# One decoder layer on one core: the indexer's queries worked out for the last 384 of 512 tokens

## The chip, the cores and the metric

The kernel runs on 1 core of a Trainium2 chip. The metric is the device time of one execution in microseconds (us); lower is better. The engines that the text speaks of are TensorE (PE in the rows; its weight loads are PEld), VectorE (DVE), ScalarE (ACT), GpSimd (POOL), and SyncE (SP), whose queue issues all loads and stores.

## The reference

One decoder layer for 512 tokens of 1024 numbers, all in float32. What the change touches is the sparse attention of branch B. An indexer scores every key for every query, and each query attends only to its best 128 keys:

```
top = min(DSA_MAX_TOPK, s // 4)                       # 128 for s = 512
logits = einsum('qhd,sd->qhs', qii, kf)               # qii: indexer queries, 8 heads of 64
score = einsum('qh,qhs->qs', wi, relu(logits))
score = where(k_pos <= q_pos, score, NEG)
_, idx = lax.top_k(score, top)
ok = idx <= q_pos
```

A query among the first 128 tokens has at most 128 admissible keys, so for it the choice takes all of them, and no score is needed. The scores of the first 128 tokens are never used.

Around it: RMSNorm and one input projection to the heads of two attention branches (MoBA in A, DSA in B), the indexer and two gates; rotary positions on all queries and keys; both attentions; a gated merge and an output projection; then a mixture of 32 experts (two of them per token) with a final RMSNorm.

## The kernel before

**First part (to about 400 us): projections and attention.** The input stands transposed in two float32r parts (`xh`, `xl`) and so do the weights (`wh`, `wl`), so one product takes three matmuls for each of 8 slices `k` (lines 255 to 257 in `proj_T`). A chunk of 256 weight columns makes two blocks of 128 rows by 512 tokens in PSUM (`two_blocks`). For queries and keys `rope_of` turns a block with four VectorE operations (lines 282 to 285), then `q_stack` copies it to a float32r part on ScalarE (line 307) and takes the rest on GpSimd (line 308). The indexer's queries are the chunks `qi0` and `qi1`, four blocks in all.

`attend` works on four quads of heads: a0, a1 (branch A), then b0, b1 (branch B). A quad has 8 steps (2 pairs of heads by 4 blocks of 128 queries). A step multiplies queries with keys (lines 432, 433), makes the softmax on VectorE and ScalarE (lines 436 to 439), transposes (448) and multiplies with the values (460). Between the pieces of a step TensorE does other work, drawn from one long list, `others()`: qi0; then qi1, qa1 and ka1 in turn with the indexer's scores (`idx_scores`, lines 389 to 393); the values vb; qb0, kb0; the merge of branch A (`merge_a`); qb1, kb1; the gates of B. How much is drawn is set by costs that each piece of the list yields (0.64 us for three projection matmuls, line 258) against the figures in `SHARE` (for a0, 9.1 us ahead of the first step and 4.4 us in each of 9). `run_to` draws what must be done before the next quad.

`topk` (lines 397 to 404) finds the 128 best keys with 16 pairs of MAX (402) and MATCH_REPLACE (403) for each of the query blocks 1, 2 and 3, 48 pairs in all on VectorE, and turns the scores (`bias1`, `bias2`, `bias3`) into a mask that b0 and b1 add to their scores (line 436).

**What sets the order.** TensorE's instructions stay in the order in which the program was written. VectorE, ScalarE, GpSimd and SP get theirs from a scheduler that estimates when each operand is ready and fills free places with later work; on the chip each queue then runs in that fixed order.

**Second part (from about 465 us): the experts.** 192 loads of 1 MB (`we`, line 609) bring all expert weights. A load can start only when one of a fixed number of places in SBUF is free; from q = 0 on a place comes free when the matmuls of its piece (lines 860, 867) are done.

Of the kernel before, what the change touches and what calls it, by code (L numbers as in the profile page):

```python
# [10 lines left out]
F32 = mybir.dt.float32  # L11
# [6 lines left out]
ALU = mybir.AluOpType  # L18
# [3 lines left out]
P = 128  # L22
T = 512
D = 1024
NT = T // P
NK = D // P
# [110 lines left out]
def layer_kernel(ctx: ExitStack, tc: tile.TileContext, xT, x, w_ki, w_ch, w_ab, w_out, g_mix, g_ffnk, g_fin, w_r, b_r,  # L137
                 w_e, const, rope, out):
    nc = tc.nc
    pe, act, dve, pool, sp = nc.tensor, nc.scalar, nc.vector, nc.gpsimd, nc.sync  # L140
# [17 lines left out]
    def t2(shape, dtype=F32, name="t2", tag="r"):  # L158
        return temps[tag][0].tile(shape, dtype, tag=tag, name=name, bufs=temps[tag][1])

    def small(shape, name, dtype=F32):
        return sm.tile(shape, dtype, tag=name, name=name)

    def bank(name="mm"):
        return pm.tile([P, 512], F32, tag="mm", name=name)
# [18 lines left out]
    def load_split(src, pair=None, place=None):  # L184
        hi, lo = pair or w_pair()
        for _ in halves_of(hi, lo, src, place):
            pass
        return hi, lo
# [15 lines left out]
    for k in range(NK):  # L204
        if k % 4 == 0:
            next(load_ki)
        r, h, l = xraw[k // 4][:, k % 4], xh[k // 4][:, k % 4], xl[k // 4][:, k % 4]
# [18 lines left out]
    cosr, sinr, cmask = rc[:, 0], rc[:, 1], rc[:, 2]  # L226
# [20 lines left out]
    def xk(k, part):  # L247
        return (xh if part == 0 else xl)[k // 4][:, k % 4]

    def proj_T(w, col, ps, ks=range(NK)):  # L250

        hi, lo = w
        for k in ks:
            a = hi[:, k, col:col + P]
            pe.matmul(ps, a, xk(k, 0), start=k == 0, stop=False)  # L255
            pe.matmul(ps, a, xk(k, 1), start=False, stop=False)  # L256
            pe.matmul(ps, lo[:, k, col:col + P], xk(k, 0), start=False, stop=k == NK - 1)  # L257
            yield 0.64

    done, due = set(), [0.0]  # L260

# [14 lines left out]
            run(gen, 0.3)  # L276
        due[0] = 0.0

    def rope_of(ps, rows=P):

        u, r = t2([rows, T], name="ru"), t2([rows, T], name="r")
        dve.tensor_tensor(r, ps, sinr[:rows], ALU.mult)
        dve.stream_shuffle(u, r, [i ^ 1 for i in range(32)])
        dve.tensor_tensor(ps, ps, cosr[:rows], ALU.mult)
        dve.tensor_tensor(r, ps, u, ALU.add)
        return r

    def chunk(name):
        with tc.high_priority(PRIO):
            return load_split(w_ch[CHUNKS.index(name)])  # L290

    def two_blocks(name):
        w, ps = chunk(name), []
        for b in range(2):
            ps.append(bank())
            yield from proj_T(w, b * P, ps[b])
        return ps

    LOW, UPP = slice(0, 64), slice(64, 128)
# [1 line left out]
    def q_stack(name, ps):  # L301

        qs = Q[name[1:]] = S.get([P, 4, T], F32R, name)
        for b in range(2):
            r = rope_of(ps[b])
            for j, h, l in ((2 * b, LOW, UPP), (2 * b + 1, UPP, LOW)):
                act.copy(qs[h, j], r[h])
                pool.tensor_tensor(qs[l, j], r[h], qs[h, j].bitcast(F32), ALU.subtract)

    def k_stack(name, ps):  # L310

# [48 lines left out]
    S.free(*xtok, junk)  # L360
    run(proj_T(w_k0, P, ps_k[1]))
    q_stack("qa0", ps_q)
    k_stack("ka0", ps_k)

# [259 lines left out]
    for n in range(4):  # L624
# [6 lines left out]
        for b in range(2):  # L631
# [11 lines left out]
            for t in range(NT):  # L643
                mv, h, l = m[:, t * P:(t + 1) * P], mt[t][:, 0, c], mt[t][:, 1, c]
# [4 lines left out]
    for a in range(0, NK, 4):  # L649
        hi, lo = [w[:, a:a + 4] for w in ws[3]]  # L650
# [240 lines left out]
    def silu_of(h1):  # L891
        out = []
        for h in range(2):
            out.append(t2([P, FF], name="silu", tag="silu"))
            act.activation(out[h], h1[h], AF.Silu)  # L895
        return out
# [111 lines left out]
    for q in range(NQ):  # L1008
        if q == last:
# [5 lines left out]
            rv = nc.values_load(cint[0:1, 0:1], min_val=0, max_val=T)  # L1015
# [12 lines left out]
        a = silu_of(h1)  # L1028
# [50 lines left out]
    for t in range(NT):  # L1079
        combine(selT, y, 1, t)  # L1080
        squares(t, 1)
        r = small([P, 1], "fin")
# [59 lines left out]
```

## Time and profile before

| | us |
|---|---|
| median of 3 runs | 941.35 (941.22 to 945.83) |
| profiled execution, its time | 942.32 |
| span of its instructions | 940.4 |
| PE busy | 875.7 |
| DVE busy | 433.8 |
| ACT busy | 278.3 |
| POOL busy | 176.5 |

The span runs from the first to the last instruction; the profiled execution took 1.9 us more than that, and 0.97 us more than the median. PE's busy time overstates its work, because one matmul starts before the one ahead has ended; what a matmul costs is read from start to start. A row of the wait view names the waiting engine and line, then the releaser, the sum, the number of waits and the longest.

### The profile page before, as it was taken

What the parts mean: (1) busy time and instruction counts of PE and PEld (TensorE: products, weight loads), DVE (VectorE), ACT (ScalarE), POOL (GpSimd) and SP (SyncE); (2) the same over time, 40 slices, a digit from 0 to 9 for tenths busy, and PEclk for the clock granted to TensorE, in tenths of its full rate; (3) what the DMA queues carried; (4) which work ended last, traced back from release to release, by engine and by line L of the source; (5) the groups of instructions that cost most, each with busy time, mean ns of one, the idle gap of its engine ahead of it and who ended that gap; (6) DMA issues with size and microseconds to landing.
All of it is one profiled execution on the core that took longest, in us unless ns stands there. A gap on an engine that the chain in (4) does not pass through costs nothing. (4 is left out here: it accounts for less than half of the span.)

```text
span 940.4 us, 15614 instructions
## 1 busy us (share of the span) xinstructions
PE 875.7 (93%) x6436; PEld 517.1 (55%) x6436; DVE 433.8 (46%) x991; ACT 278.3 (30%) x585; POOL 176.5 (19%) x112
## 2 busy tenths in 40 slices
PE   7999999989999999889999999998998989987885
PEld 5897779768777877689834342422423223232221
DVE  4737899998544545941823322231322212213004
ACT  5546654562444544433501000000100000100004
POOL 2495334342214711221200000000000000000003
PEclk9999999999999999899999999999999999999898
DMA  8422112112224223455679999999999999999985
GB/s 330 157 71 67 55 36 90 48 57 77 77 82 180 87 69 112 135 229 228 226 317 421 419 420 421 420 418 422 419 420 420 421 422 419 421 420 419 402 327 217
DMA packets 41118, 244.51 MB, mean 260 GB/s; under 512 B 4944, under 2 KB 5328, under 8 KB 16336
## 3 DMA queue, kind: packets, MB, share of 16 engines
q1 hardware_dynamic: 41040, 243.45, 65.0%
q8 instruction: 52, 0.85, 0.4%
q14 instruction: 26, 0.21, 0.1%
HBM read 241.33 MB, written 2.10 MB: 259 GB/s over the span
## 5 line engine op out<-in xcount | busy, mean ns | idle before, releaser
L860 PE MATMUL h<-we,xs 128*32 128x512 f32 x2048 | 238.4, 601 | 26.3 <-DMA we<-in_w_e_dram 19.4
L860 PEld LDWEIGHTS h<-we,xs 128*32 128x32 f32 x2048 | 59.1, 110 | 180.5 <-issue 117.4
L867 PE MATMUL y<-we,hT 128*32 128x512 f32 x1024 | 116.3, 595 | 5.3 <-DMA we<-in_w_e_dram 5.2
L255 PE MATMUL mm<-xh,wh 128*128 128x512 f32 x272 | 109.9, 404 | 0.8 <-DVE bias L393 0.8
L257 PE MATMUL mm<-xh,wl 128*128 128x512 f32 x272 | 107.5, 395 | 0.0
L256 PE MATMUL mm<-xl,wh 128*128 128x512 f32 x272 | 107.5, 395 | 0.0
L1072 POOL TENSOR_TENSOR fo<-x,gfn 128x512 f32<-128x512 f32 x4 | 5.0, 1282 | 450.0 <-DVE x L927 450.0
L170 POOL TENSOR_TENSOR wl<-raw,wh 128x1024 fp32r<-128x1024 f32 (+1 forms) x23 | 64.5, 2803 | 132.1 <-ACT wh L169 68.5
L927 DVE TENSOR_TENSOR x<-cps,x 128x512 f32<-128x512 f32 x64 | 43.3, 688 | 86.3 <-PE cps L925 86.1
L867 PEld LDWEIGHTS y<-we,hT 128*32 128x32 f32 x1024 | 30.0, 109 | 77.1 <-issue 57.0
L901 DVE SCALAR_TENSOR_TENSOR silu<-silu,gate,h 128x512 f32<-128x512 f32 x16 | 12.0, 747 | 124.5 <-issue 82.8
L257 PEld LDWEIGHTS mm<-xh,wl 128*128 128x128 f32 x272 | 51.1, 188 | 12.6 <-DVE wl L170 0.4
L255 PEld LDWEIGHTS mm<-xh,wh 128*128 128x128 f32 x272 | 51.1, 188 | 11.7 <-issue 1.2
L256 PEld LDWEIGHTS mm<-xl,wh 128*128 128x128 f32 x272 | 51.2, 188 | 9.5
L169 ACT CAST wh<-raw 128x1024 fp32r<-128x1024 f32 (+1 forms) x46 | 45.6, 1028 | 31.9 <-DMA raw<-in_w_ch_dram 13.5
L169 ACT CAST y<-y 128x512 fp32r<-128x512 f32 x32 | 18.8, 586 | 121.7 <-PE y L867 121.7
L908 ACT COPY hT<-htr 128x512 f32<-128x512 f32 x16 | 8.7, 589 | 150.2 <-PE htr L906 150.2
L895 ACT ACTIVATE silu<-h 128x512 f32<-128x512 f32 x16 | 9.6, 598 | 145.1 <-PE h L860 145.1
L170 DVE TENSOR_TENSOR y<-y,y 128x512 fp32r<-128x512 f32 x32 | 22.0, 689 | 62.9 <-ACT y L169 62.8
L437 ACT ACTIVATE ps<-e,st 128x128 f32<-128x128 f32 (+3 forms) x64 | 33.5, 524 | 43.9 <-DVE st L436 43.6
L170 DVE TENSOR_TENSOR wl<-raw,wh 128x1024 fp32r<-128x1024 f32 (+1 forms) x23 | 31.9, 1389 | 26.9 <-ACT wh L169 22.3
L677 PE MATMUL mm<-woh,mt 128*128 128x256 f32 x128 | 37.4, 293 | 0.0
(201 smaller groups left out, 1570.7 us busy)
## 6 DMA issues: line engine op xcount, KB each, us to landing
we<-in_w_e_dram SPq DMA_DIRECT2D x192, 1024.0 KB, 19.8
raw<-in_w_ch_dram SPq DMA_DIRECT2D x44, 512.0 KB, 4.1
raw<-in_w_ab_dram SPq DMA_DIRECT2D x8, 512.0 KB, 4.1
raw<-in_w_out_dram SPq DMA_DIRECT2D x6, 512.0 KB, 4.2
xraw<-in_xT_dram SPq DMA_DIRECT2D x8, 256.0 KB, 5.8
xtok<-in_x_dram SPq DMA_DIRECT2D x4, 512.0 KB, 9.1
x<-in_x_dram SPq DMA_DIRECT2D x4, 512.0 KB, 5.1
out_dram<-fo SPq DMA_DIRECT2D x8, 256.0 KB, 2.3
```

The lines of the kernel that those rows point to most:

```text
L169: act.copy(hi, raw)
L170: eng.tensor_tensor(lo, raw, hi.bitcast(F32), ALU.subtract)
L255: pe.matmul(ps, a, xk(k, 0), start=k == 0, stop=False)
L256: pe.matmul(ps, a, xk(k, 1), start=False, stop=False)
L257: pe.matmul(ps, lo[:, k, col:col + P], xk(k, 0), start=False, stop=k == NK - 1)
L437: act.activation(ps[:, :n], e[:, :n], AF.Exp, bias=st[:, 0:1], scale=-1.0, accum_out=st[:, 1:2])
L677: pe.matmul(ps, a, hi[:, k], start=k == 0, stop=False)
L860: pe.matmul(ps[h][CAP * e:CAP * (e + 1)], xs[:, k, h, CAP * e:CAP * (e + 1)], w[:, e * FF:(e + 1) * FF], start=k == 0, stop=k == NK - 1)
L867: pe.matmul(ys[h][CAP * e:CAP * (e + 1)], hT[h][:, k, CAP * e:CAP * (e + 1)], w[:, e * FF:(e + 1) * FF], start=k == 0, stop=k == 3)
L895: act.activation(out[h], h1[h], AF.Silu)
L901: dve.scalar_tensor_tensor(a[h], a[h], gate[:, h:h + 1], h3[h], ALU.mult, ALU.mult)
L927: dve.tensor_tensor(o, ps, o, ALU.add)
```

## The change

For the chunks whose name begins with `qi`, the first token is now 128 instead of 0. Their projections read and write columns 128 to 511 only (matmuls of 384 columns), the rotation, the copy and the subtraction work on these 384 columns, and the cost that the projection yields to the list falls from 0.64 to 0.48. All other chunks keep their 512 columns. The number of instructions is unchanged on every engine. The diff:

```
-    def proj_T(w, col, ps, ks=range(NK)):
+    def proj_T(w, col, ps, ks=range(NK), t0=0):
 
         hi, lo = w
         for k in ks:
-            a = hi[:, k, col:col + P]
-            pe.matmul(ps, a, xk(k, 0), start=k == 0, stop=False)
-            pe.matmul(ps, a, xk(k, 1), start=False, stop=False)
-            pe.matmul(ps, lo[:, k, col:col + P], xk(k, 0), start=False, stop=k == NK - 1)
-            yield 0.64
+            a, xhi, xlo, o = hi[:, k, col:col + P], xk(k, 0)[:, t0:], xk(k, 1)[:, t0:], ps[:, t0:]
+            pe.matmul(o, a, xhi, start=k == 0, stop=False)
+            pe.matmul(o, a, xlo, start=False, stop=False)
+            pe.matmul(o, lo[:, k, col:col + P], xhi, start=False, stop=k == NK - 1)
+            yield 0.64 * (T - t0) / T
...
-    def rope_of(ps, rows=P):
-
-        u, r = t2([rows, T], name="ru"), t2([rows, T], name="r")
-        dve.tensor_tensor(r, ps, sinr[:rows], ALU.mult)
-        dve.stream_shuffle(u, r, [i ^ 1 for i in range(32)])
-        dve.tensor_tensor(ps, ps, cosr[:rows], ALU.mult)
-        dve.tensor_tensor(r, ps, u, ALU.add)
+    def rope_of(ps, rows=P, t0=0):
+
+        u, r, ps = t2([rows, T], name="ru")[:, t0:], t2([rows, T], name="r"), ps[:, t0:]
+        rv = r[:, t0:]
+        dve.tensor_tensor(rv, ps, sinr[:rows, t0:], ALU.mult)
+        dve.stream_shuffle(u, rv, [i ^ 1 for i in range(32)])
+        dve.tensor_tensor(ps, ps, cosr[:rows, t0:], ALU.mult)
+        dve.tensor_tensor(rv, ps, u, ALU.add)
         return r
...
+    def first_token(name):
+
+        return P if name[:2] == "qi" else 0
+
     def two_blocks(name):
         w, ps = chunk(name), []
         for b in range(2):
             ps.append(bank())
-            yield from proj_T(w, b * P, ps[b])
+            yield from proj_T(w, b * P, ps[b], t0=first_token(name))
         return ps
...
         for b in range(2):
-            r = rope_of(ps[b])
+            t0 = first_token(name)
+            r = rope_of(ps[b], t0=t0)
             for j, h, l in ((2 * b, LOW, UPP), (2 * b + 1, UPP, LOW)):
-                act.copy(qs[h, j], r[h])
-                pool.tensor_tensor(qs[l, j], r[h], qs[h, j].bitcast(F32), ALU.subtract)
+                act.copy(qs[h, j, t0:], r[h, t0:])
+                pool.tensor_tensor(qs[l, j, t0:], r[h, t0:], qs[h, j, t0:].bitcast(F32), ALU.subtract)
```

Because the list's costs fall and `SHARE` does not, the attention of a0 draws more of the list, and from there on the same work stands earlier in TensorE's order. Two places show it; behind the change the lines from 299 on have moved down by 6 (432 is 438, 436 is 442).

**TensorE around the first scores of a0 and of the indexer.** `mm` is a projection block (here of qi1), `tp` the transposed weights of the indexer's heads, `ips` a score block of the indexer, `ps` one of a0. Before, a0's first scores stood 9 projection matmuls ahead of `tp`, and its second scores followed the first score block of the indexer:

```order
L257 MATMUL mm<-xh_96,wl 128x512
L389 MATMUL ips<-kst_364,qi_19_690 128x256
L390 MATMUL ips<-kst_364,qi_19_690 128x256
L255 MATMUL mm<-xh_97,wh 128x512
L256 MATMUL mm<-xl_99,wh 128x512
L257 MATMUL mm<-xh_97,wl 128x512
L432 MATMUL ps<-hika_13_334,qa_12_313 128x256
L433 MATMUL ps<-loka_14_335,qa_12_313 128x256
```

Now a0's first scores follow the transposes at once:

```order
L386 MATMUL tp<-cb,wie 128x128 x4
L438 MATMUL ps<-hika_13_334,qa_12_313 128x256
L439 MATMUL ps<-loka_14_335,qa_12_313 128x256
L438 MATMUL ps<-hika_13_334,qa_12_313 128x256
L439 MATMUL ps<-loka_14_335,qa_12_313 128x256
L255 MATMUL mm<-xh_96,wh 128x384
L256 MATMUL mm<-xl_98,wh 128x384
L257 MATMUL mm<-xh_96,wl 128x384
```

What moved: 54 projection matmuls of 384 columns now stand ahead of a0's first scores, where 45 of 512 stood, and by the second scores 3 score blocks of the indexer are issued, where 1 was. Each step of a0, a1 and b0 keeps its share of other work, by cost. At the end, 42 projection matmuls stand between the last values of b0 and the first scores of b1, where 66 stood; from these scores on TensorE's order is the same in both.

**VectorE in a1, between its sixth and seventh step.** `bias_379` is bias2 and `bias_380` bias3, `e` a softmax, `r` and `mm` the rotation of a block, `wl` the low part of a weight chunk. Before:

```order
L403 MATCH_REPLACE bias_379<-m_2142,bias_379 128x384
L403 MATCH_REPLACE bias_380<-m_2146,bias_380 128x512
L282 TENSOR_TENSOR r<-mm,rc 128x512
L439 TENSOR_SCALAR e<-ps,st 128x256 x2
L284 TENSOR_TENSOR mm<-mm,rc 128x512
L404 TENSOR_SCALAR bias_379<-bias_379 128x384
L170 TENSOR_TENSOR wl<-raw,wh 128x1024
L402 MAX m_2149<-bias_380 128x8
L283 STREAM_SHUFFLE ru<-r 128x512
L436 ISA e,st<-ps,rc 128x384
```

Now, in the same place:

```order
L442 ISA e,st<-ps,rc 128x256
L442 ISA st 128x1
L408 MAX m_2186<-bias_380 128x8
L444 RECIPROCAL st<-st 128x1 x2
L409 MATCH_REPLACE bias_380<-m_2186,bias_380 128x512
L445 TENSOR_SCALAR e<-ps,st 128x256 x2
L408 MAX m_2189<-bias_380 128x8
L283 TENSOR_TENSOR r<-mm,rc 128x512
```

What moved: the mask operation (404) and the weight split (170) no longer stand in this step, and bias2 is finished earlier. Counted over the whole order, 23 of the 48 MAX operations stand ahead of a1's first softmax, where 19 stood; 25 stand between it and b0's first softmax, where 28 stood; of the weight splits (170), 12 where 11 stood and 5 where 6 stood. By b0's first softmax VectorE has one MAX, two MATCH_REPLACE, the mask operation of bias3 and one gate product (486) more behind it than before. GpSimd keeps its order. On SP the last two of the four loads of `x2` (line 584) now follow two weight loads that they preceded.

## Rows read from the trace of the kernel before

**Rows 1.** The page: busy time of each engine, and four lines of the span in 40 equal slices (23.5 us each), busy share in tenths.

```profile
PE 875.7 (93%) x6436; PEld 517.1 (55%) x6436; DVE 433.8 (46%) x991; ACT 278.3 (30%) x585; POOL 176.5 (19%) x112
...
PE   7999999989999999889999999998998989987885
...
DVE  4737899998544545941823322231322212213004
...
PEclk9999999999999999899999999999999999999898
DMA  8422112112224223455679999999999999999985
```

**Rows 2.** Busy time by stretch: start and end, length, then PE, PEld, DVE, ACT and POOL busy us with the number of instructions, granted clock, DMA share, GB/s.

```profile
60.00:114.00 54.00, 52.15 (x285) 41.61 (x284) 39.80 (x98) 31.48 (x70) 28.37 (x17) 1.00 0.21 69
114.00:150.00 36.00, 33.25 (x233) 28.51 (x232) 35.10 (x95) 20.79 (x41) 19.22 (x12) 1.00 0.17 59
150.00:195.00 45.00, 39.56 (x264) 32.57 (x263) 44.05 (x125) 21.37 (x55) 12.64 (x8) 1.00 0.21 71
195.00:225.00 30.00, 30.00 (x157) 23.96 (x156) 28.25 (x59) 15.79 (x25) 14.36 (x10) 1.00 0.17 54
225.00:318.00 93.00, 93.00 (x481) 73.80 (x480) 49.52 (x115) 40.40 (x82) 30.57 (x14) 1.00 0.29 102
```

**Rows 3.** TensorE in order of time: start us, us, then the instruction. The first and the last of 25 matmuls of 256 columns of the values' projection; the first and the last of 45 matmuls of qi0; a score block of the indexer of 384 columns and the matmul two places behind its start.

```profile
57.76 0.28 PE L336 MATMUL mm<-wh,xl 128*128 128x256 f32 x1
...
60.58 0.28 PE L336 MATMUL mm<-wh,xl 128*128 128x256 f32 x1
60.70 0.39 PE L255 MATMUL mm<-xh,wh 128*128 128x512 f32 x1
...
70.97 0.40 PE L257 MATMUL mm<-xh,wl 128*128 128x512 f32 x1
...
88.99 0.34 PE L389 MATMUL ips<-kst,qi 128*128 128x384 f32 x1
...
89.35 0.39 PE L255 MATMUL mm<-xh,wh 128*128 128x512 f32 x1
```

**Rows 4.** Groups of VectorE instructions of one shape between 60 and 240 us: line, operation, names, shapes, count, then busy us, mean ns of one, and idle time before them with what ended it.

```profile
L170 DVE TENSOR_TENSOR wl<-raw,wh 128x1024 fp32r<-128x1024 f32 x10 | 15.9, 1588 | 10.1 <-ACT wh L169 9.1 <-PE mm L257 0.9
L402 DVE MAX8 m<-bias 128x8 f32<-128x512 f32 x16 | 11.0, 685 | 0.2
L403 DVE MATCH_REPLACE8 bias<-m,bias 128x512 f32<-128x512 f32 x16 | 10.8, 674 | 0.0
...
L282 DVE TENSOR_TENSOR r<-mm,rc 128x512 f32<-128x512 f32 x12 | 8.2, 684 | 2.3 <-PE mm L257 2.2
...
L402 DVE MAX8 m<-bias 128x8 f32<-128x256 f32 x16 | 6.8, 422 | 0.3
...
L393 DVE SCALAR_TENSOR_TENSOR bias<-ips,wi,bias 128x512 f32<-128x512 f32 x7 | 5.2, 741 | 0.3 <-ACT ips L391 0.2
...
L393 DVE SCALAR_TENSOR_TENSOR bias<-ips,wi,bias 128x384 f32<-128x384 f32 x7 | 4.3, 610 | 1.2 <-ACT ips L391 1.1
...
L486 DVE TENSOR_TENSOR g<-mm,rbc 128x512 f32<-128x512 f32 x4 | 2.7, 686 | 0.3 <-PE mm L257 0.3
```

**Rows 5.** Waits of TensorE's matmuls between 60 and 240 us: all that are listed for PE itself.

```profile
PE ps L432 <- DVE e L439: 5.4, 4, 2.1
...
PE ips L389 <- DVE bias L393: 3.0, 5, 1.3
...
PE ips L389 <- DVE wi L381: 0.8, 1, 0.8
PE mm L255 <- DVE bias L393: 0.8, 1, 0.8
```

**Rows 6.** The indexer's queries on ScalarE and GpSimd (the view of the tile `qi`): count, then duration in ns (least, median, most), first and last start in us, shapes.

```profile
L307 ACT CAST qi<-r x8: 611/618/622, 69.3 to 96.8; 64x512 fp32r<-64x512 f32 x8
L308 POOL TENSOR_TENSOR qi<-r,qi x8: 1271/1286/1292, 70.0 to 98.3; 64x512 fp32r<-64x512 f32 x8
```

**Rows 7.** Weight loads of TensorE that go with matmuls of 256 columns (335) and of 512 (257), from the view of the tile `wl`, same columns.

```profile
L335 PEld LDWEIGHTS mm<-wl,xh x72: 187/187/189, 38.1 to 139.7; 128*128 128x128 f32 x72
...
L257 PEld LDWEIGHTS mm<-xh,wl x66: 187/188/188, 24.8 to 135.6; 128*128 128x128 f32 x66
```

**Rows 8.** Later stretches, columns as in rows 2: two at a lower granted clock, one between them at the full one, one more at a lower clock, and the experts.

```profile
385.00:390.00 5.00, 2.15 (x6) 1.56 (x6) 5.00 (x11) 2.44 (x8) 0.92 (x1) 0.68 0.62 220
390.00:395.00 5.00, 5.00 (x16) 3.96 (x15) 4.83 (x10) 2.54 (x6) 1.52 (x1) 0.64 0.21 76
...
405.00:410.00 5.00, 5.00 (x44) 5.00 (x43) 1.36 (x7) 0.51 (x3) 3.48 (x1) 1.00 0.06 14
...
415.00:420.00 5.00, 5.00 (x35) 5.00 (x35) 0.42 (x1) 1.26 (x4) 0.00 (x0) 0.75 1.00 423
...
480.00:930.00 450.00, 417.42 (x3642) 140.69 (x3634) 112.94 (x184) 39.31 (x71) 5.00 (x4) 0.99 0.99 409
```

**Rows 9.** Waits of SP's queue between 380 and 480 us: loads of expert weights that wait for a free place.

```profile
SPq L609 <- PE mm L679: 47.4, 6, 13.8
SPq L609 <- PE h L860: 13.1, 2, 12.6
```

**Rows 10.** GpSimd in order of time: the low part of the second half of chunk qi0.

```profile
60.87 2.40 POOL L170 TENSOR_TENSOR wl<-raw,wh 128x1024 fp32r<-128x1024 f32 x1
```

## The prediction

> **What bounds the kernel now.** I read the busy time by slices first, then by stretch, then TensorE's waits, and the expert stage last.
>
> TensorE is the fullest engine at 875.7 us, but from the 21st slice (about 470 us) on the DMA digits are at 9 to the end [rows 1]: from 480 to 930 us the DMA engines are busy for 0.99 of the time [rows 8]. That stage is bound by loading 192 MB, and nothing in the change touches it. It starts, however, when SBUF places come free, and what frees them is TensorE: the loads wait 47.4 us for matmuls of line 679 and 13.1 us for the first ones of line 860 [rows 9]. So if TensorE arrives there earlier, the loads start earlier by as much and so does the end. The question is how much earlier.
>
> Ahead of it there are two kinds of stretch. Up to 114 us TensorE is nearly full (52.15 of 54.00) and VectorE is not (39.80). From 114 to 195 us VectorE is full, 35.10 of 36.00 and 44.05 of 45.00, and TensorE has gaps of 2.75 and 5.44 us. From 195 on TensorE is full again: 30.00 of 30.00, then 93.00 of 93.00, with VectorE at 28.25 and at 49.52 [rows 2]. The gaps are waits for VectorE: 5.4 us of a1's scores for the softmax, and 3.0, 0.8 and 0.8 us around the indexer's scores, 10.0 us in all [rows 5]. A microsecond of TensorE's work is therefore worth a microsecond where TensorE is full, and may be worth nothing between 114 and 195 us.
>
> **TensorE's saving.** Four blocks of 8 slices by 3 products are 96 matmuls, from 512 to 384 columns. From start to start a matmul of 512 columns takes (70.97 - 60.70) / 44 = 0.2334 us, one of 256 takes (60.58 - 57.76) / 24 = 0.1175, and the two of 384 take (89.35 - 88.99) / 2 = 0.18 [rows 3]. A straight line between 256 and 512 gives 0.1755 for 384. Saving: 96 x (0.2334 - 0.1755) = 5.6 us, or 96 x (0.2334 - 0.18) = 5.1 us by the indexer's own pair, which also holds a change of operands. I take the line, since the 96 run one behind the other, and keep 5.1 as the lower end.
>
> The Trainium skill has a formula for this (TensorE: Matmul & The Clock Gate, section "Wait — 56ns, not 53.3ns?"): N columns take N / 2.4 GHz plus about 2.5 ns at the full clock. That makes 215.8 and 162.5 ns and a saving of 5.1 us. The row for 512 columns has 233.4 ns, 8% more, so here the measurement decides.
>
> **Where it is saved.** Not where the matmuls stand. The yielded cost falls with them, and the list is drawn by cost, so every step of a0, a1 and b0 keeps its length on TensorE and simply gets further down the list. The balance shows in the order ahead of b1: 42 projection matmuls where 66 stood, 24 x 0.2334 = 5.6 us. That place lies inside 225 to 318 us, where TensorE is full, and from there on its order is the same. So the 5.6 us are gained where nothing else is the bound, provided that a0, a1 and b0 take as long as before. What could change their length is VectorE.
>
> **VectorE.** Saved: 16 operations of the rotation, each by a quarter of its columns. The indexer's operation shows the step from 512 to 384: 741 - 610 = 131 ns, and a rotation operation of 512 takes 684, much the same [rows 4]; so 16 x 0.131 = 2.1 us. Pulled forward to before b0's first softmax: one MAX (0.685), two MATCH_REPLACE (1.35), a gate product (0.686) [rows 4] and a mask operation of at most as much, 3.4 us. Net, 1.3 us more for VectorE in the same time on TensorE. Between 60 and 225 us VectorE has 165 - 147.2 = 17.8 us idle (the first four of rows 2 summed), most of it ahead of 114 us, where the indexer's scores now come earlier and take it up. In the full part, from a1's first softmax to b0's, the order has three MAX, two MATCH_REPLACE and a split less, and a gate product and a mask more: 2.1 + 1.3 + 1.6 - 0.7 - 0.7 = 3.6 us less at the durations of rows 4, less than that since more of those that stay are the wide ones of bias3. So a1 should wait less for VectorE, a0 more: its indexer scores are denser (3 ahead of the second step where 1 was). I take both as cancelling, 0, with -3.0 and +3.5 us as ends: the relief of a1 nearly whole, or all that is pulled forward showing as waits.
>
> **At no cost.** ScalarE's 8 copies and GpSimd's 8 subtractions (618 and 1286 ns [rows 6]) become shorter; neither engine is waited for in rows 5, so no gain is counted. GpSimd's split of the second half of qi0 ends at 63.27 us [rows 10]; TensorE would want it after 12 + 2 matmuls, at 60.70 + 14 x 0.1755 = 63.2, so the cover of that load is gone and up to 0.1 to 0.3 us may show once. The two loads of x2 that fall behind two weight loads on SP are first read by line 681, after all attention.
>
> **Clock.** Two stretches of the later part run at a lower granted clock, 0.68 and 0.64 from 385 to 395 us, where TensorE was busy for 2.15 of 5 us, and 0.75 from 415 to 420 [rows 8], levels of 1.2 and 2.4 GHz mixed. The second did 35 matmuls where a full one did 44, 1.0 us lost. All later work arrives 5.6 us earlier against whatever sets this, so one such drop may go or another come: 1.0 us either way.
>
> **Sum**, against the profiled execution: 942.32 - 5.6 + 0 = 936.7. That execution took 0.97 us more than the median, so the forecast for the median is 941.35 - 5.6 = 935.75, say 935.8 us.
>
> **Rivals.**
>
> *A, VectorE takes part of it back.* It is full from 114 to 195 us, and one more heap of work, of the kind that made one wait of 2.1 us [rows 5], costs as much. After the change the stretches ahead of a0's last step and of a1's fourth and sixth hold rotations and MAX pairs together, as that ahead of a1's seventh did before. With waits 1.3 to 3.5 us longer: 941.35 - 5.6 + 1.3 = 937.1 to 939.3. For it: a saturated engine. Against it: VectorE's own sum in that part falls.
>
> *B, the waits shrink too.* The long wait in a1 goes with its heap (mask operation and split leave that step), and of a1's 5.4 us of waits 3.0 go: 935.75 - 3.0 = 932.8. For it: the 3.6 us fewer. Against it: fixed orders made from estimates usually find a new place to wait.
>
> *C, slower.* The indexer's scores in a0 need a PSUM bank that VectorE's line 393 frees, and its queue is fixed. If a MAX (0.422 [rows 4]), which the scheduler now places earlier, stands ahead of each of the 24 accumulations and TensorE waits for it each time, that costs 24 x 0.42 = 10.1 us: 941.35 - 5.6 + 10.1 = 945.9. The sign turns at 5.6 / 24 = 0.23 us more per score block. Now 24 blocks wait 4.6 us in all, 0.19 each [rows 5], so they would have to wait more than twice as much; and the MAX operations that move forward are only four.
>
> *D, the matmuls don't shrink in proportion.* A weight load of 128 columns takes 188 ns [rows 7], more than 175. If loads set the pace the saving is 96 x (0.2334 - 0.188) = 4.4 us: 937.0. Against it: the values' matmuls of 256 columns, each with a load of 187 ns, follow one another every 0.1175 us.
>
> **How the numbers follow.** The forecast, with waits about as before, 0.50; A 0.20; B 0.22; D 0.03; C 0.05. About half a per cent, 4.7 us, is what a measurement of this kernel can tell from no change: faster means below 936.6, slower above 946.1. Of the forecast's 0.50, whose own spread is 934.4 to 937.2, I put 0.33 below 936.6 and 0.17 above. Faster: 0.33 + 0.22 = 0.55. Same: 0.17 + 0.20 + 0.03 and most of C = 0.42. Slower: the upper part of C, 0.03. Range: B and a clock drop less, 932.8 - 1.0 = 931.8, to A's upper end and a clock drop more, 939.3 + 1.0 = 940.3; so 932.0 to 940.3.
>
> **What would show it.** Right: 96 matmuls of 384 columns about 0.176 us apart; the first scores of b0 (line 432 before) at the same time as before, give or take 3 us, the first scores of b1 some 5.6 us earlier; the loads' last stage as long as before and ending earlier by as much. A shows as longer waits of line 432 or 389 for VectorE than 10.0 us in all; B as shorter ones; C as waits of line 389 above 10 us; D as a spacing of 0.188. The forecast is wrong in its main step if the gain at b1's first scores is there and the end does not follow it, for then the start of the expert loads is set by something other than TensorE.

## The result, and the profile after

| | before | after |
|---|---|---|
| median, runs on the same chip in turn | 941.35 us (13 runs, 938.27 to 945.83) | 946.92 us (13 runs, 942.80 to 949.00) |
| profiled execution, its time | 942.32 us | 947.34 us |
| span of its instructions | 940.4 us | 944.9 us |

The ratio is 1.0052, with a 95% interval of 1.0033 to 1.0071: the change makes the kernel slower by about half a per cent. It was forecast to be 5.6 us faster. The same file, timed once more in a later session (e9 below), came to 1.0029 (1.0004 to 1.0053).

The matmuls themselves do what was forecast. TensorE in order of time (start us, us, instruction), from the projection of qi0, answers to [rows 3]:

```profile
65.83 0.34 PE L257 MATMUL mm<-xh,wl 128*128 128x384 f32 x1
...
70.51 0.34 PE L257 MATMUL mm<-xh,wl 128*128 128x384 f32 x1
```

27 matmuls of 384 columns lie between the two starts: (70.51 - 65.83) / 27 = 0.1733 us each, where 0.1755 was taken. So 96 x (0.2334 - 0.1733) = 5.8 us are saved. The same view shows where they go. The first scores of a0's fourth step, of b0 and of b1, before:

```profile
90.73 0.50 PE L432 MATMUL ps<-hika,qa 128*128 128x512 f32 x1
...
223.16 0.28 PE L432 MATMUL ps<-hikb,qb 128*128 128x256 f32 x1
...
317.51 0.28 PE L432 MATMUL ps<-hikb,qb 128*128 128x256 f32 x1
```

and after:

```profile
98.20 0.50 PE L438 MATMUL ps<-hika,qa 128*128 128x512 f32 x1
...
232.97 0.28 PE L438 MATMUL ps<-hikb,qb 128*128 128x256 f32 x1
...
321.71 0.28 PE L438 MATMUL ps<-hikb,qb 128*128 128x256 f32 x1
```

From b0 to b1 the lag falls from 9.81 to 4.20 us: 5.6 us are gained exactly where the prediction put them. This fall shows the order, 24 projection matmuls fewer ahead of b1, and not by itself a saving: e4 below, which saves nothing, has nearly the same (8.68 to 3.28 us). The span ends 4.5 us later, so the end follows b1's first scores. But b0 starts 9.8 us late, and most of that lag is there by a0's fourth step, at 7.5 us.

The table by stretch (start and end, length, busy us of PE, PEld, DVE, ACT, POOL with their instructions, granted clock, DMA share, GB/s) answers to [rows 2]:

```profile
60.00:114.00 54.00, 49.02 (x276) 41.39 (x275) 37.75 (x89) 28.85 (x64) 25.68 (x17) 0.94 0.20 69
...
225.00:318.00 93.00, 93.00 (x481) 73.80 (x480) 49.27 (x109) 40.18 (x79) 26.52 (x14) 1.00 0.30 102
```

In the last row TensorE and its clock are as before. The first is the one that broke: TensorE 49.02 where it was 52.15, and a granted clock of 0.94 where it was 1.00 (1.00 is 2.4 GHz, 0.50 is 1.2 GHz). TensorE's waits between 60 and 240 us answer to [rows 5] (engine and line, releaser, sum, number, longest):

```profile
PE ps L438 <- DVE e L445: 4.3, 3, 2.6
PE ips L395 <- DVE r L286: 3.3, 1, 3.3
PE mm L255 <- DVE bias L399: 2.5, 2, 1.8
PE ips L395 <- DVE bias L399: 2.1, 3, 1.6
PE ops L466 <- ACT pt L456: 1.1, 2, 0.6
PE ips L395 <- DVE wi L387: 0.4, 1, 0.4
PE ips L395 <- POOL qi L314: 0.3, 1, 0.3
```

They sum to 14.0 where 10.0 stood, and 3.3 of it is one wait that did not exist: an indexer block waits for the rotation of qi1's last block. All engines in order of time around it:

```profile
84.06 2.00 ACT L169 CAST wh<-raw 128x1024 fp32r<-128x1024 f32 x2
...
85.73 0.58 DVE L284 STREAM_SHUFFLE ru<-r 128x384 f32<-128x384 f32 x1
...
86.19 2.37 POOL L170 TENSOR_TENSOR wl<-raw,wh 128x1024 fp32r<-128x1024 f32 x1 [4.42 <-PE ps L439]
86.21 3.42 DVE L170 TENSOR_TENSOR wl<-raw,wh 128x1024 fp32r<-128x1024 f32 x1
...
89.56 0.54 DVE L442 CUSTOM_DVE_ANT_0 e<-ps,rc 128x384 f32<-128x384 f32 x1
...
90.51 0.55 DVE L286 TENSOR_TENSOR r<-mm,ru 128x384 f32<-128x384 f32 x1
...
91.11 0.80 PE L395 MATMUL ips<-kst,qi 128*128 128x512 f32 x1 [3.25 <-DVE r L286]
```

ScalarE casts both halves of chunk ka1 one after the other, to 86.06. GpSimd's half of the low part starts at 86.19, VectorE's at 86.21, and VectorE's takes 3.42 us, where the same operation takes 1.2 when nothing holds it. GpSimd is done at 88.56; 89.63 is 1.07 us later, about one undisturbed half. So VectorE's operation seems to have stood still until GpSimd's was over; e1, e2 and e5 below test that. Two softmax operations and the rotation (286) are queued behind it, and TensorE waits for the rotation. Then the clock goes (same columns as the stretches above):

```profile
85.00:90.00 5.00, 2.86 (x16) 2.09 (x12) 5.00 (x6) 1.53 (x3) 2.37 (x1) 1.00 0.00 0
90.00:95.00 5.00, 3.88 (x11) 3.21 (x12) 3.58 (x11) 3.40 (x9) 2.00 (x2) 0.55 0.59 213
95.00:100.00 5.00, 5.00 (x23) 3.59 (x23) 1.78 (x4) 0.82 (x2) 0.00 (x0) 0.77 0.00 0
```

TensorE was busy for 2.86 of 5 us, and the next 10 us run partly at 1.2 GHz: (1 - 0.55) x 5 + (1 - 0.77) x 5 = 3.4 us less of the full clock. Not all of it is lost time, since TensorE still waits for 1.11 of these 10 us. From the matmul behind the wait to a0's fourth scores it takes 98.20 - 91.11 = 7.09 us, and the same stretch takes 4.25 at the full clock (e1 and e2 below), so the clock costs 2.8 us there. Wait and clock together are 6.1 us, more than the 5.8 saved.

### The profile page after: what moved, and what is told of

Read it like the earlier page. It is cut to its first block, busy times and chain, and to the rows that moved or that the text cites. A ratio compares the mean times of both kernels' runs of the same rounds, so it can differ in the third digit from the quotient of the medians.

```text
span 944.9 us, 15628 instructions
## 1 busy us (share of the span) xinstructions
PE 874.7 (93%) x6436; PEld 518.3 (55%) x6436; DVE 433.9 (46%) x991; ACT 277.5 (29%) x585; POOL 172.2 (18%) x112
## 5 line engine op out<-in xcount | busy, mean ns | idle before, releaser
L255 PE MATMUL mm<-xh,wh 128*128 128x512 f32 (+1 forms) x272 | 109.6, 403 | 2.5 <-DVE bias L399 2.5
L256 PE MATMUL mm<-xl,wh 128*128 128x512 f32 (+1 forms) x272 | 106.3, 391 | 0.0
L257 PE MATMUL mm<-xh,wl 128*128 128x512 f32 (+1 forms) x272 | 106.2, 390 | 0.0
L170 DVE TENSOR_TENSOR wl<-raw,wh 128x1024 fp32r<-128x1024 f32 (+1 forms) x23 | 35.7, 1553 | 31.5 <-ACT wh L169 22.7
```

What stands on the lines that cost most here:

```text
L170: eng.tensor_tensor(lo, raw, hi.bitcast(F32), ALU.subtract)
L255: pe.matmul(o, a, xhi, start=k == 0, stop=False)
L256: pe.matmul(o, a, xlo, start=False, stop=False)
L257: pe.matmul(o, lo[:, k, col:col + P], xhi, start=False, stop=k == NK - 1)
```

## The experiments

Theory 1 is this collision. Rival 2 is the prediction's own: VectorE is too full in general once the indexer's scores come earlier. Rival 3 is a clock that falls there anyway. "b1" below is the start of b1's first scores in the profiled execution against 317.51 before; the ratio is that of the medians to the kernel before on the same chip.

| run | median us | ratio (95%) | b1, us |
|---|---|---|---|
| the change | 946.92 | 1.0052 (1.0033 to 1.0071) | +4.20 |
| e9 the change again | 945.53 | 1.0029 (1.0004 to 1.0053) | +3.83 |
| e1 ka1's halves both on GpSimd | 938.38 | 0.9971 (0.9947 to 0.9996) | -2.55 |
| e2 ka1's halves swapped | 942.03 | 0.9993 (0.9972 to 1.0015) | +0.36 |
| e3 columns only | 940.55 | 0.9981 (0.9960 to 1.0002) | -3.30 |
| e4 order only | 944.96 | 1.0032 (1.0010 to 1.0054) | +3.28 |
| e5 GpSimd's half in pieces | 942.54 | 0.9988 (0.9968 to 1.0008) | +4.63 |
| e6 wait filled with zeros | 941.17 | 0.9983 (0.9969 to 0.9997) | +3.95 |
| e7 columns, two splits moved | 935.00 | 0.9923 (0.9898 to 0.9948) | -5.96 |
| e8 columns, all splits moved | 932.11 | 0.9895 (0.9871 to 0.9919) | -6.43 |
| e10 before, all splits moved | 937.64 | 0.9949 (0.9932 to 0.9966) | -3.38 |
| e11 the change, all splits moved | 938.17 | 0.9960 (0.9941 to 0.9978) | -2.09 |
| e12 columns, splits from qa1 moved | 931.32 | 0.9881 (0.9854 to 0.9907) | -9.99 |
| e13 as e11, first draw lowered | 938.82 | 0.9956 (0.9938 to 0.9974) | -1.63 |
| e14 as e11, scores less dense | 940.68 | 0.9981 (0.9964 to 0.9998) | -0.77 |

### The collision: e1, e2, e5, e9

**e1** gives VectorE no half of ka1.

```
-            split(hi[:, a:a + 4], lo[:, a:a + 4], raw, pool if a else dve)
+            split(hi[:, a:a + 4], lo[:, a:a + 4], raw, (engs or (dve, pool))[a // 4])
...
-            return load_split(w_ch[CHUNKS.index(name)])
+            return load_split(w_ch[CHUNKS.index(name)], engs=(pool, pool) if name == "ka1" else None)
```

> The changed kernel, except that both halves of the weight split of chunk ka1 are GpSimd's (VectorE has no half of it). Theory 1, the collision (VectorE's half was held for 3.42 us because GpSimd's half had started 0.02 us ahead, TensorE then waited 3.25 us and its granted clock fell for 6.8 us): the wait of TensorE for the rotation after ka1's split falls from 3.25 us to under 0.5, the granted clock stays at 1.0 between 85 and 105 us, and the time falls by 3.2 + 3.4 = 6.6 us to about 940.3 (939.3 to 941.5). Rival 2, a VectorE that is too full over the whole stretch: only the 1.2 us of the half itself come back, 945 to 946. Rival 3, a clock that falls at this place whatever is waited for: 943.5.

Measured: 938.38 us, 0.9 below the range that was expected, and b1's first scores 6.75 us earlier than in the change (314.96 for 321.71), against 6.6 expected. Of the 6.75, 0.54 is there by the third scores of a0 (84.61 for 85.15), ahead of the collision; from the third to the fourth the change takes 6.2 us more (98.20 - 85.15 for 91.48 - 84.61), and that is what the edit gives back. In order of time, e1:

```profile
84.70 4.77 POOL L170 TENSOR_TENSOR wl<-raw,wh 128x1024 fp32r<-128x1024 f32 x2 [3.46 <-ACT wh L169]
...
85.68 0.54 DVE L442 CUSTOM_DVE_ANT_0 e<-ps,rc 128x384 f32<-128x384 f32 x1
...
86.62 0.55 DVE L286 TENSOR_TENSOR r<-mm,ru 128x384 f32<-128x384 f32 x1
...
87.23 0.50 PE L395 MATMUL ips<-kst,qi 128*128 128x512 f32 x1
...
91.48 0.50 PE L438 MATMUL ps<-hika,qa 128*128 128x512 f32 x1
```

Softmax and rotation run while GpSimd is busy and take their usual 0.54 and 0.55 us; TensorE's matmul does not wait. The granted clock is 1.00 from 85 to 100 us. Rival 2 expected 1.2 us and falls as the main cause.

**e2** swaps the two halves. On VectorE the two softmax operations come ahead of the half; nothing else moves on any engine.

```
-            return load_split(w_ch[CHUNKS.index(name)])
+            return load_split(w_ch[CHUNKS.index(name)], engs=(pool, dve) if name == "ka1" else None)
```

> The changed kernel, except that GpSimd takes the first half of ka1's split and VectorE the second; on VectorE the two softmax operations that stood behind the half now stand ahead of it, and no other instruction of any engine moves. GpSimd can start after ScalarE's first cast, 1 us earlier, so it should end near 87.5 us, and VectorE's half, which starts behind the softmax at about 87.2, should end near 88.6 where it ended at 89.6. Theory 1: TensorE waits about 1.5 us where it waited 3.25; the time is 945 if the granted clock falls as before, 941.8 if it does not. Rival 2: less than 1 us is won, 946 or more. Rival 3: the clock falls, 945.

Measured: VectorE's half starts at 86.75 and takes 1.57 us, TensorE waits 1.40 us (1.5 expected), the clock stays at 1.00 there, and the fourth scores start at 93.09 where they started at 98.20: 5.1 us, of which 0.4 is there by the third scores (84.73 for 85.15), 1.85 is wait and 2.84 is clock. Later in this execution the clock fell at another place:

```profile
185.00:190.00 5.00, 4.09 (x14) 3.36 (x15) 4.94 (x17) 2.52 (x6) 2.57 (x2) 0.66 0.60 202
```

That costs 0.34 x 5 = 1.7 us, so b1 shows less than a0 did. 942.03 us fits the expectation without the fall (941.8).

**e5** cuts GpSimd's half of ka1 into four operations; all other engines keep their order.

```
+        for c in range(0, 4, step):
+            s = slice(c, c + step)
+            eng.tensor_tensor(lo[:, s], raw[:, s], hi[:, s].bitcast(F32), ALU.subtract)
```

> The changed kernel, except that GpSimd's half of ka1's split is cut into four operations of 256 columns; every instruction of the other engines stands where it stood. Theory 1 (VectorE's half waits for the GpSimd operation that runs when it comes, not for a lack of room on VectorE): it is held for one piece of about 0.6 us instead of 2.35 us, ends about 1.7 us earlier, TensorE waits 1.5 us in place of 3.25, the granted clock does not fall near 90 us, and the time is about 941 to 943. If VectorE is held behind all four pieces, nothing changes: 946 to 948. Rival 2, VectorE too full: at most 1 us is won, 946.

Measured, in order of time (lines are 4 higher from here on in the file, 399 is the indexer's matmul):

```profile
87.32 3.78 POOL L174 TENSOR_TENSOR wl<-raw,wh 128x256 fp32r<-128x256 f32 x4 [4.41 <-PE ps L443]
87.35 1.80 DVE L171 TENSOR_TENSOR wl<-raw,wh 128x1024 fp32r<-128x1024 f32 x1
...
90.62 0.50 PE L399 MATMUL ips<-kst,qi 128*128 128x512 f32 x1 [1.63 <-DVE r L290]
```

GpSimd is ahead again, by 0.03 us, but VectorE is held by one piece only: 1.80 us for 3.42. TensorE waits 1.63 us, the clock stays at 1.00 from 85 to 100 us, and from the third to the fourth scores of a0 the lag grows by 1.4 us where it grew by 5.9 in the change. The median is 942.54, as expected. Its profiled execution reached b1 no earlier than the change, since the clock fell in two later places, to 0.82 and 0.84 from 120 to 130 us and to 0.81 and 0.51 from 185 to 195:

```profile
190.00:195.00 5.00, 5.00 (x15) 3.84 (x14) 3.48 (x11) 1.54 (x6) 1.76 (x2) 0.51 0.19 79
```

**e9** is the change unaltered, to see whether a lead of 0.02 us falls out the same way twice.

> The changed kernel once more, unaltered. Theory 1 as a fixed meeting: GpSimd's half of ka1's split starts first again, VectorE's half takes some 3.4 us, TensorE waits 3.2 us, and the time is 946 to 948. Rival 5, a race that falls out either way (the lead was 0.02 us): VectorE starts first in this execution, its half takes 1.2 us, TensorE waits under 0.5 us and the fourth scores of a0 come at about 91.5 us where they came at 98.2.

```profile
85.67 2.37 POOL L170 TENSOR_TENSOR wl<-raw,wh 128x1024 fp32r<-128x1024 f32 x1 [4.40 <-PE ps L439]
85.70 3.43 DVE L170 TENSOR_TENSOR wl<-raw,wh 128x1024 fp32r<-128x1024 f32 x1
...
90.61 0.50 PE L395 MATMUL ips<-kst,qi 128*128 128x512 f32 x1 [3.27 <-DVE r L286]
```

It does: GpSimd leads by 0.03 us and VectorE's half takes 3.43; the median is 945.53 for 946 to 948 expected. Only the clock differs: 0.67 from 90 to 95 us and 0.99 after, 1.7 us less of the full clock instead of 3.4. One of its 12 runs took 937.57 us, the others 942.21 to 949.13; whether the race went the other way in that one isn't known, since it has no profile. So small a lead in the recorded starts does not decide who holds whom. In e3 below GpSimd's half of ka1 is recorded first too, by 0.02 us, and there it is GpSimd's that is held and VectorE's that takes its 1.21 us; e7 shows the same:

```profile
87.90 3.48 POOL L170 TENSOR_TENSOR wl<-raw,wh 128x1024 fp32r<-128x1024 f32 x1 [4.74 <-ACT wh L169]
87.92 1.21 DVE L170 TENSOR_TENSOR wl<-raw,wh 128x1024 fp32r<-128x1024 f32 x1
```

### The clock: e6

14 matmuls by a tile of zeros stand in the place of the wait. They add nothing to the sums.

```
+            for _ in range(14 if k == fill else 0):
+                pe.matmul(o, a, zero, start=False, stop=False)
```

> The changed kernel with 14 more TensorE matmuls of 512 columns that multiply by a tile of zeros, added to the block of qa1 just ahead of the indexer's score block that waited 3.25 us; 14 x 0.234 = 3.3 us of work in the place of the wait, the sums unchanged. The split collides as before. If the clock falls because TensorE stood idle, it stays at 1.0 between 85 and 100 us, a0's fourth scores come 3.4 us earlier than in the changed kernel (about 94.8 us), and the time is about 943.5. If the clock falls there for another reason (rival 3), the fourth scores stay at about 98.2 us and the time at 947. If the added matmuls delay what VectorE waits for, it is 950.

Measured, in order of time (lines are 5 higher here, 400 is the indexer's matmul) and by stretch:

```profile
86.55 3.44 DVE L170 TENSOR_TENSOR wl<-raw,wh 128x1024 fp32r<-128x1024 f32 x1
...
88.03 3.43 PE L261 MATMUL mm<-zero,wh 128*128 128x512 f32 x14
...
91.47 0.50 PE L400 MATMUL ips<-kst,qi 128*128 128x512 f32 x1
```

```profile
85.00:90.00 5.00, 5.00 (x26) 4.07 (x26) 5.00 (x7) 1.87 (x3) 2.39 (x1) 1.00 0.01 3
90.00:95.00 5.00, 4.99 (x24) 3.59 (x22) 4.46 (x12) 3.84 (x10) 2.02 (x2) 1.00 0.60 210
```

The collision is there as before (3.44 us), and with TensorE kept at work through it the clock does not fall. The fourth scores of a0 start at 95.72 (94.8 expected, 98.20 in the change). From the third to the fourth scores of a0 this kernel takes 10.24 us, the change 13.06: the 2.8 us of the clock are back, and the wait is filled, not shortened. Useless work in an idle place made the kernel faster than the change: 0.9983 for 1.0052, 941.17 us where 943.5 was expected. Rival 3 falls. The ratio gives more than this fall of the clock costs; VectorE's order also differs from 121 us on in this kernel, and the clock fell at 125 and at 190 us instead (0.66 each), so only the place near 90 us is shown by it.

### Columns and order apart: e3, e4

**e3** keeps the list's cost at 0.64, so TensorE's order is that of before, with 384 columns for qi:

```
-            yield 0.64 * (T - t0) / T
+            yield 0.64
```

**e4** is the opposite: the cost falls to 0.48 and all 512 columns are worked out.

```
-            a, xhi, xlo, o = hi[:, k, col:col + P], xk(k, 0)[:, t0:], xk(k, 1)[:, t0:], ps[:, t0:]
+            a, xhi, xlo, o = hi[:, k, col:col + P], xk(k, 0), xk(k, 1), ps
...
-            t0 = first_token(name)
-            r = rope_of(ps[b], t0=t0)
+            t0 = 0
+            r = rope_of(ps[b], t0=t0)
```

> The changed kernel with the list's cost left at 0.64 for the indexer's queries, so that 384 columns are worked out in the order that TensorE had before the change. Theory 1: the 5.6 us of the 96 matmuls are won unless the shorter work brings the two halves of some split to the same moment; 936 to 938 without such a meeting, 940 to 943 with one. Rival 2, VectorE too full because indexer scores were moved ahead: they are not moved here, so 936 to 938. Rival 4, 384 columns that save nothing by themselves: 941.

> The changed kernel with all 512 columns worked out again, so that only the lower cost (0.48) and the order drawn from it differ from the kernel before. Theory 1: nothing is saved, and the order costs something only where it makes a split collide; 941 to 943 if ka1's halves do not start together, 946 to 949 if they do. Rival 2, VectorE too full by the denser order: 945 to 948 without any half of a split being held and with TensorE waiting for the indexer's sums instead.

Measured: e3 is 4.60 us ahead at a1's first scores and 3.30 at b1's; between them the clock fell once (0.66 from 190 to 195 us, 1.7 us), so the columns are worth 5.0 us of TensorE's time by this trace. The medians show 0.9981, or 1.8 us, with an interval that reaches from none to 3.8; the mean granted clock of its runs has a median of 0.983 where before has 0.985, and an estimate of up to 0.002 x 940 = 1.9 us of the rest is that. The 940.55 us of e3 lie in the range expected of a meeting, but its trace has the same three held halves as before (2.35, 2.04 and 3.00 us) and no new one. e4 is 3.28 us behind at b1, with no collision (VectorE's half of ka1 starts 0.39 us ahead of GpSimd's and takes 1.21) and the clock at 1.00 up to 320 us. So the order costs some 3 us by itself, where 941 to 943 us was expected without a collision; TensorE's listed waits hold little of it (10.7 us for 10.0; 1.1 of the 10.7 are two waits for ScalarE's `pt` that before does not have, and the indexer's sums are waited for 4.9 us for 3.8, so rival 2 is not ruled out for a part of this cost). Columns, order and collision together, -5.0 + 3.3 + 6.2 = +4.5, against +4.20 measured.

### Without shared splits: e7, e8, e10, e11, e12

If held splits are what costs, VectorE should have none of them where it is full. The edit is that of e1 with another condition:

```
+            return load_split(..., engs=(pool, pool) if name in ("vb1", "qb0") else None)
...
+            return load_split(..., engs=(pool, pool) if name[:2] not in ("va", "gb") else None)
...
+            return load_split(..., engs=(pool, pool) if name[:2] not in ("va", "gb", "qi") else None)
```

e7 is e3 with the first line; e8 is e3 with the second, e10 the kernel before and e11 the change with the second; e12 is e3 with the third.

> The kernel of 384 columns with the list's cost left at 0.64, and both halves of the splits of vb1 and qb0 on GpSimd; on VectorE these two were held to 2.04 and 3.00 us, and TensorE waited 1.98 us behind the second (for a block of the values). Theory 1: the held operations and that wait go, 2 us less than with the columns alone at b1's first scores, and 938 to 939 in all; if the clock's fall near 190 us goes too, 936 to 937. Rival 2: the scheduler fills VectorE's places with other work and the wait turns up elsewhere, 940 to 941 as with the columns alone.

> The kernel of 384 columns with the list's cost left at 0.64, and both halves of all weight splits from qi0 to kb1 and of branch A's gates on GpSimd, so that VectorE has none of them and none can be held. Theory 1: VectorE is rid of some 13 operations of 1.2 to 3.0 us, waits of TensorE for softmax and indexer sums shrink, 935 to 938. The other way: GpSimd needs 2.4 us for a half, two halves follow one another, and weights come late; TensorE waits for a low part (wl) and the time is 943 or more.

> The kernel before (512 columns), with both halves of all weight splits from qi0 to kb1 and of branch A's gates on GpSimd. Against the same move with 384 columns (932.1 us), it gives what the 384 columns save where no split is held: 937 to 938 if it is the 5.6 us of the matmuls; 932 to 934 if the gain of that kernel came from the splits alone and the columns save nothing; 943 if the splits' move gains only with the shorter queries.

> The changed kernel (384 columns, lower cost in the list), with both halves of all weight splits from qi0 to kb1 and of branch A's gates on GpSimd. If the order drawn from the lower cost costs some 3 us by itself, as the order alone did (1.0032 of the kernel before), it is 935 to 936; if that cost came only of held splits, it equals the kernel with the cost left at 0.64, 932; if GpSimd now delivers the first weights too late for an order that asks earlier for them, 938 or more.

> 384 columns, the list's cost left at 0.64, and both halves of the splits on GpSimd from qa1 to kb1 and for branch A's gates; the splits of qi0 and qi1 stay shared. With those two on GpSimd as well, TensorE waited 3.0 us for the low part of qi and 1.2 us for a low part of the weights. If these waits came of GpSimd's longer queue, they go, and the time is 928 to 930; if VectorE's two halves (held to 1.9 and 2.3 us in all kernels so far) take as much back, 932.

Measured: e7 935.00 us, below all that was expected. At b1 it is 2.7 us ahead of e3, with one fall of the clock near 190 us in both profiles; by the medians 5.5, part of which is the clock (median of the runs' mean granted clocks 0.9875 for 0.983). e8 932.11, below what was expected too. In it TensorE waits for GpSimd instead (waits from 60 to 240 us):

```profile
PE ips L395 <- POOL qi L314: 3.0, 1, 3.0
...
PE mm L257 <- POOL wl L170: 1.2, 1, 1.2
```

Behind the wait of 3.0 us the clock fell in e8 (0.66 from 80 to 85 us).

e12 leaves GpSimd the time for qi's low part:

```profile
PE ips L395 <- POOL qi L314: 1.7, 1, 1.7
```

It is the fastest of all, 931.32 us or 0.9881 of the kernel before, and beats both kernels, though not by the whole of what was looked for (928 to 930); the medians don't separate it from e8 (0.9895). Moving the splits is worth (1 - 0.9949) x 942 = 4.8 us in the kernel before (e10), nearly as much as the columns. e10 against e8 gives the columns' own worth where the splits are out of VectorE's way: 937.64 - 932.11 = 5.5 us by the medians, 5.1 by the ratios, for 5.6 forecast; at b1 it is 3.0, with the fall of the clock in e8 that e10 does not have. And e11 against e8, 938.17 - 932.11 = 6.1 us (4.3 at b1), is the order's cost in this company, more than the 3.3 of e4. The 938.17 us of e11 are what was expected if GpSimd delivers too late for this order, but TensorE's wait for qi's low part is 3.7 us for 3.0 in e8, so that is a small part at most. Against e10, in the same session, the change with its splits moved wins nothing (0.9960 for 0.9949): the order takes back what the columns give.

### What the order costs: e13, e14

Both start from e11. e13 lowers the first draw of a0; e14 mixes the indexer's scores into the list by cost.

```
-SHARE = {"a0": (9.1, 4.4), ...
+SHARE = {"a0": (6.8, 4.4), ...
...
-            owed += share
+            owed += 1.1 * share * c / 0.64
```

> The changed kernel with all splits from qi0 to kb1 on GpSimd (938.2 us in its own run, 0.9960 of the kernel before), and the list's first draw for a0 lowered from 9.1 to 6.8, so that 45 projection matmuls stand ahead of a0's first scores, as before the change, and 1 indexer block ahead of the second step. If the order's cost came of the larger first draw, 3 to 4 us come back at b1's first scores, 934 to 935; if it came of the denser indexer scores later in a0, less than 1 us, 937 to 938.

> The changed kernel with all splits from qi0 to kb1 on GpSimd, and the indexer's scores mixed into the list by cost instead of by pieces: by the third step of a0 6 score blocks are issued where 7 were, by the fourth 9 where 10 were; the first draw stays. If the order's cost came of the denser scores, 2 us or more come back, 936 or less; if it came of the first draw, nothing, 938.

Measured: 938.82 and 940.68 us; both lie above all that was expected, and neither is below e11 (938.17), so neither the larger first draw nor the denser scores is shown as the cause. In e13 the clock fell for longer in a0 than in e11 (0.95, 0.50 and 0.86 in the three stretches from 75 to 90 us), which hides up to 1.7 us, not the 4 that were looked for. What makes that order slower stays open.

## Why the prediction was wrong

- **TensorE's saving, 5.6 us: right.** 0.1733 us a matmul gives 5.8, and e10 against e8 gives 5.5 by the medians. Rival D (188 ns by the weight loads) is refuted.
- **Where it is saved: right in place.** 9.81 to 4.20 us of lag between b0 and b1. But the condition, that a0, a1 and b0 take as long as before, did not hold, and without it this place says nothing of a saving (e4: 8.68 to 3.28).
- **The end follows TensorE: right.** +4.20 us at b1, +4.5 at the end.
- **VectorE, "I take both as cancelling, 0": the step that failed.** It counted which operations moved and priced each at its mean. The split's mean of 1588 ns in [rows 4] was no price at all: it mixes seven halves of 1.2 us with three that were held to 2.0, 2.3 and 3.0. VectorE's half costs 1.2 us when it goes first and up to 3.4 behind a GpSimd operation, and the new order put the two starts of ka1 0.02 us apart, GpSimd's ahead, with TensorE's next operand behind it. That was 3.25 us of wait and 2.8 of clock, at the term that stood at 0. e1 takes this half from VectorE and regains 6.2 us between a0's third and fourth scores; e5, which moves no instruction of another engine, regains 4.5 there. No sum of the prediction could tell that the starts would fall so close together; that halves can be held was there to read in the kernel before. The ends of the range, -3.0 to +3.5, came from the same sums and did not hold it.
- **"Neither engine is waited for in rows 5, so no gain is counted": wrong as an argument.** GpSimd is not named in the wait of 3.25 us either, the rotation is; but it was GpSimd's operation that held VectorE. The Trainium skill states the rule (SBUF — State Buffer, section "Who interferes with whom"): a VectorE instruction with two inputs from SBUF and a GpSimd instruction that reads SBUF exclude one another, and whichever starts first runs to its end. Here the trace agrees: 2.35 us of GpSimd's rest and 1.07 of its own make the 3.42. For starts that are recorded 0.02 us apart it does not show which of the two goes first (e3 and e7).
- **Clock, 1.0 us either way: wrong in place and size.** Only the later stretches of [rows 8] were looked at. The fall that mattered came in a0 behind the new wait, 2.8 us, and e6 shows that it goes when TensorE is kept busy there.
- **The order at no cost of its own: wrong by some 3 us** (e4). Rival A, VectorE taking 1.3 to 3.5 back, has this size, but the cause of the order's cost is not shown. The sign that A named did come in the change, 12.6 us of waits for VectorE where 10.0 stood, but 3.3 of them are the held split's.
- **Rival C had the sign but not the mechanism.** TensorE's waits for the indexer's sums (`bias`) are 2.5 + 2.1 = 4.6 us, where [rows 5] had 3.0 + 0.8 = 3.8; the 10 us of that rival did not come.

The check that the prediction set itself, b0's first scores at the same time give or take 3 us, is the one that failed, by 9.8.

## What to carry to other kernels

Where two engines share halves of one job, read the single durations, not the mean: some far above the rest (2.0 to 3.0 us beside 1.2 here) are a sign that one engine holds the other, and that any edit which moves either start can turn a hidden half into a stall. Price a move with both values, and ask who stands behind the held operation. If the slower engine has room, give it both halves: that was worth 0.5% with the old columns (e10) and made the new ones pay in the old order (e8, e12).

An edit that lowers a cost in a work list is two edits, the work and the order; run them apart before believing either. And a new wait of TensorE is priced with the clock behind it: 3.25 us of waiting cost 2.8 us more.

## What the runs showed of the hardware that was not expected

**Which VectorE operations are held.** Above all those with two inputs from SBUF. In e1 a softmax operation (one input from PSUM) and a rotation take 0.54 and 0.55 us under a running GpSimd split. At 398 us of the changed kernel an operation of 128 columns with both inputs in SBUF takes nine times its usual 0.28 us:

```profile
398.00 3.18 POOL L170 TENSOR_TENSOR wol<-raw,woh 128x1024 fp32r<-128x1024 f32 x1 [7.74 <-ACT woh L169]
398.82 2.52 DVE L652 SCALAR_TENSOR_TENSOR mt<-ma,mt 128x128 fp32r<-128x128 f32 x1
...
402.86 0.28 DVE L652 SCALAR_TENSOR_TENSOR mt<-ma,mt 128x128 fp32r<-128x128 f32 x1
```

One operation with a single tensor input in SBUF, beside one number per partition, is held too: the multiplication of line 361 at 29.0 us, under a GpSimd split from 28.94 to 31.37 us (count, then duration in ns, least, median and most):

```profile
L361 DVE TENSOR_SCALAR dg<-cb,rstd x4: 275/276/2426, 29.0 to 31.8; 128x128 f32<-128x128 f32 x4
```

**The hold ends with the instruction, not with the queue.** In e5 VectorE got in after the first of four GpSimd operations (1.80 us in place of 3.42). Cutting GpSimd's work into smaller operations bounds the hold to one of them.

**The clock after a wait is not the same in every execution.** After the same wait of 3.3 us the granted clock was short of the full one by 3.4 us in one execution and by 1.7 in another (the change, e9), and by nothing after waits of 1.40 and 1.63 us at that place (e2, e5). Near 190 us the clock fell in e2, e3, e5, e6, e7 and e9, and not in the change or in e1; the two later falls of e5 are 5.1 us of the full clock. So executions of one kernel differ by a few us in this way alone, and an edit of a few us is judged by many runs, and by the times at which fixed places in the program are reached.
